# Moving four of the six modulation sums of each layer ahead of its attention heads

## The chip, the cores and the metric

One core of one Trainium2 chip. The metric is device time in microseconds (us) of one execution. Before the change: 3334.44 us, the median of 3 runs (3331.59 to 3336.16).

## The reference

Two layers, each with a token-mixing half (a stick-breaking branch and an MLA branch, 8 heads each) and a squared-ReLU MLP. S = 1024 positions, D = 1024 channels, float32. What the change touches is `mod`, six vectors of 1024 numbers per layer:

```python
for l in range(DEPTH):                                  # 2
    mod = (c_act @ w_ada[l] + b_ada[l])[:, None, :]     # (1024,) @ (1024, 6144)
    shift1, scale1, gate1, shift2, scale2, gate2 = jnp.split(mod, 6, axis=-1)
    h = _rms_norm(x, g_mix_norm[l]) * (1.0 + scale1) + shift1
    p = h @ w_in[l]                                     # q, k, v, latents, rope, gates
    ...                                                 # both attention branches
    x = x + gate1 * (merged @ w_mix_out[l])
    h = _rms_norm(x, g_mlp_norm[l]) * (1.0 + scale2) + shift2
    x = x + gate2 * (jnp.square(jax.nn.relu(h @ w_up[l])) @ w_down[l])
```

So vectors 0 and 1 are needed at the start of a layer, 2 (gate1) after its heads, 3 to 5 in its MLP. `w_ada` is 24 MB per layer, each vector 4 MB.

## The kernel before

The activations are held transposed, channels on partitions. Every product of two float32 operands is made of three passes (high x high, high x low, low x high parts), each a matmul of a 128x128 weight tile with 512 columns, into the PSUM banks `pp`. One layer runs, in program order, through these stages: the latent projections (`lraw`, `lt`); the stretch ahead of the heads, called so below (the rope key, the first q, k, v pair, gates 0 to 3, then in `for p in range(4)` the up-projections from the latents to the heads' q, k, v, and gates 4 to 7); the stick-breaking heads (scores `sc<-sq`); the MLA heads (`sc<-mq`); the output products and the mixing product (`merged`); the up-projection, a pair loop with fast products on half blocks (`pw`, results in `u`); the down-projection (`bo`, `ws`, sums in `x`).

The order on each engine isn't the program's. The code records all operations in a `Plan`; `Plan.deadlines` gives each a due time worked back from TensorE's program order, and `Plan.schedule` is a list scheduler over five engines (TensorE, ScalarE, VectorE, GpSimd, one DMA queue on SyncE) with its own durations, which writes the order out. Tiles of one class take its buffers strictly in the order in which the program makes them (`c.tiles[j] is not t` in `slots_for`). All instructions are recorded by one helper, so every row of the profile has line L213, and work is told apart by tile names.

The modulation. VectorE, not TensorE, sums `w_ada` rows weighted by the activated c: `modulation(l, parts)` is a generator that goes through the given vectors in blocks of 256 columns. A block has four loads of 256 KB into `AD` (2 buffers), two multiply-adds each into `acc` (class `A`, 3 buffers, 128 partitions x 256), eight in all, with one step of the generator per load. `finish` splits the sum into a high part (ScalarE) and a low part (GpSimd), both in class `A` too, and sums over partitions by four matmuls with two columns of ones into a bank of class `tp`, which VectorE adds to `mod`. The heads use the two `tp` banks for their transposes and outputs, and the latents' norm uses them ahead of that. The first layer's vectors 0 and 1 are made in `start` by other code (tile `ada`). Before, layer 0's vectors 2 to 5 (16 blocks, 128 multiply-adds) are stepped by `interleave`, among the heads of layer 0, and all six of layer 1 (24 blocks, 192 multiply-adds) among the pair loop and the down-projection of layer 0. Layer 1 itself carries none.

Evictions ahead of the heads: `keep_split` writes a high part (ScalarE) and a low part (VectorE) into two `lt` tiles (4 buffers, class `lt2`) and stores both; `keep` writes a `T` tile (ScalarE) and stores it; `rope` has six VectorE operations. `load_w` loads 128 columns of a weight into `raw`, ScalarE and GpSimd split it into `parts`.

Of the kernel before, what the change touches and what calls it, by code (L numbers as in the profile page):

```python
# [25 lines left out]
DEPTH = 2  # L26
# [460 lines left out]
class Trunk:  # L487
# [631 lines left out]
    def layer(self, l, xT, ssq, before):  # L1119
# [17 lines left out]
        def gate(m):  # L1137
            gd[m] = self.dt([P, S])
            return (win_w(2208 + m * P), self.keep(gd[m], AF.Sigmoid if m < 8 else AF.Copy), P)
# [23 lines left out]
        def rope(ps, sl, n, out):  # L1163

            a, b = ltmp(), ltmp()
            nc.vector.tensor_mul(a, ps, cos[:, sl])
            nc.vector.tensor_mul(b[:64], ps[64:], sin[64:, sl])
            nc.vector.tensor_mul(b[64:], ps[:64], sin[:64, sl])
            nc.vector.tensor_add(a, a, b)
            hi, lo = ltmp(F32R), ltmp(F32R)  # L1170
            nc.scalar.copy(out=hi, in_=a)
            nc.vector.tensor_sub(lo, a, bc(hi))
            for i, t in enumerate((hi, lo)):
                for r in (0, 64) if n < 64 else (0,):
                    m = n if n < 64 else P
                    o = r // 64 * n
                    nc.sync.dma_start(out=out[i, o : o + m, sl], in_=bc(t[r : r + m]))
# [56 lines left out]
        lat_norm(0, range(0, 3), QR, "g_q_lat")  # L1234
        lat_norm(1, range(3, 5), KVR, "g_kv_lat")
        kr_job = (kr_w, lambda ps, sl: rope(ps, sl, 16, kpe_d), P)
        for _ in self.linear([kr_job] + qkv(0) + [gate(m) for m in range(4)], hh, hl, KT):
            pass

        c_qp, c_lt = self.vcls("qp", 16, 17, *range(18, 24)), self.vcls("lt2", 15, 5, 6, 7)  # L1240

# [26 lines left out]
        for p in range(4):  # L1268
            mq[p], mk[p], mv[p] = self.two(), self.two(), self.dt([P, S])
            if p % 2 == 0:  # L1270
                wq = q_parts(p // 2)
            q_w = part(wq, p % 2 * P)
            for _ in self.linear([(q_w, self.keep_split(mq[p], ltmp), P)], lath, latl, 3):
                pass
            wkv = kv_parts(p)
            k_w, v_w = part(wkv, 0), part(wkv, P)
            kv_jobs = [(k_w, self.keep_split(mk[p], ltmp), P), (v_w, self.keep(mv[p]), P)]
            for _ in self.linear(kv_jobs, lath[3:], latl[3:], 2):
                pass
            if p % 2 == 0:  # L1280
                g = p // 2
                qr_d[g] = self.two()
                w = part(wq, 2 * P)()
                for sl in HALVES:
                    ps = self.bank("pp")
                    self.mm3(ps, w, lath, latl, sl, 3)
                    rope(ps, sl, 64, qr_d[g])
            for _ in self.linear([gate(4 + p)], hh, hl, KT):
                pass

        self.attention_banks()

# [67 lines left out]
        fill = [self.linear(qkv(p + 1), hh, hl, KT) for p in range(3)]  # L1360
        fill += [self.linear([gate(m) for m in range(8, 16)], hh, hl, KT)]
        fill = self.chain(fill)
        ada = self.modulation(0, [2, 3, 4, 5]) if l == 0 else iter(())
        for name, head, weights, mask, vals, steps in (
            ("sb", sb_head, self.sb_weights, self.mask_s, vd, SB_STEPS),
            ("mla", mla_head, self.mla_weights, self.mask_c, mv, MLA_STEPS),
        ):
            if name == "sb":
                self.c_q, self.c_F = self.vcls("sq", *q_slots[:6]), self.vcls("F", *q_slots[6:])
            else:  # L1370
                self.c_q = self.vcls("mq", *q_slots)
                fill = self.chain([fill, sb_out()])
            for p in range(4):
                od[name, p] = self.dt([P, S])
                a = self.attend([head(p, e) for e in range(2)], lambda: self.make_v(vals[p]), weights, mask, od[name, p])
                self.interleave(a, 19, fill, steps[p], ada)
        for _ in self.chain([fill, ada]):
            pass


# [61 lines left out]

        NP = DFF // P // 2
        hid = [self.dt([P, 8, HALF]) for m in range(NP)]
        ada = self.modulation(l + 1, range(6)) if l + 1 < DEPTH else iter(())

        def hidden(f):
            where = (0, 7) if f % 2 == 0 else (1, 2)
# [23 lines left out]
        for m in range(2, DFF // P // 2):  # L1472
            a, S3, c, d, S1, S2, S4 = self.pair_weights(I["w_up"][l, :, 2 * m * P : 2 * (m + 1) * P], c_pr, c_pw)
            u, v = self.full(c_u), self.full(c_u)
            next(ada, None)
            p1 = self.product(a, B11)
            nc.scalar.copy(out=u[:, :HALF], in_=p1)
            p6 = self.product(S2, T[2])
            nc.vector.tensor_add(u[:, HALF:], p6, u[:, :HALF])
            next(ada, None)  # L1480
            p7 = self.product(S3, T[3])
            nc.vector.tensor_add(v[:, :HALF], p7, u[:, HALF:])
            p5 = self.product(S1, T[1])
            nc.vector.tensor_add(v[:, HALF:], p5, v[:, :HALF])
            nc.vector.tensor_add(u[:, HALF:], p5, u[:, HALF:])
            next(ada, None)
            p4 = self.product(d, T[4])
            nc.vector.tensor_sub(v[:, :HALF], v[:, :HALF], p4)
            p2 = self.product(c, B21)
            nc.vector.tensor_add(u[:, :HALF], p2, u[:, :HALF])  # L1490
            next(ada, None)
            p3 = self.product(S4, B22)
            nc.vector.tensor_add(u[:, HALF:], p3, u[:, HALF:])
            for t in (v, u):
                nc.scalar.activation(out=t, in_=t, func=AF.Relu)
                nc.scalar.activation(out=t, in_=t, func=AF.Square)
            nc.sync.dma_start(out=hid[m][:, 0], in_=u[:, :HALF])
            nc.sync.dma_start(out=hid[m][:, 1:3], in_=v.rearrange("p (a b) -> p a b", a=2))
            combine(m, u, v)
            if m in (3, 5):  # L1500
                u, v = self.full(c_u), self.full(c_u)
                i = m // 2 - 1
                nc.sync.dma_start(out=u[:, :HALF], in_=hid[i][:, 0])
                nc.sync.dma_start(out=u[:, HALF:], in_=hid[i][:, 7])
                nc.sync.dma_start(out=v.rearrange("p (a b) -> p a b", a=2), in_=hid[i][:, 1:3])
                combine(i, u, v)
        ssq = [self.tmp(), self.tmp()]
        steps = self.down(l, hid, x_d, ssq)
        for _ in range(48):
            next(steps)  # L1510
            next(ada, None)
        for _ in ada:
            pass
        return self.xT, ssq, steps

    def down(self, l, hid, x_d, ssq):
# [111 lines left out]
            yield from g  # L1628

    @staticmethod  # L1630
    def interleave(a, na, b, nb, c):

        done = 0
        for i, _ in enumerate(a):
            if i % 2 == 1:
                next(c, None)
            want = (i + 1) * nb // na
            while done < want:
                next(b, None)
                done += 1  # L1640
# [69 lines left out]
```

## Time and profile before

| | |
|---|---|
| median of 3 runs | 3334.44 us |
| profiled execution | 3345.88 us |
| its span (first to last instruction) | 3344.1 us |
| TensorE busy | 3116.7 us, 93% |
| VectorE busy | 2295.3 us, 69% |
| ScalarE, GpSimd busy | 1544.1 us, 1243.2 us |
| multiply-adds of `modulation` | 320 on VectorE, from 160 loads |

The profile is of one execution; times in it are from its span's start. Busy time says how long an engine had an instruction under way; what a stage is bound by is seen from the engine that never pauses in it, and from the waits. PE is TensorE's matmuls, PEld its weight loads, DVE VectorE, ACT ScalarE, POOL GpSimd, SPq the queue of SyncE, which issues all DMAs.

### The profile page before, as it was taken

The numbers are of one execution on the slowest core, as the hardware profiler recorded it, in microseconds if no ns is written. First come the engines' busy times: TensorE is split into PE (matmuls) and PEld (weight loads), VectorE is DVE, ScalarE is ACT, GpSimd is POOL, SyncE is SP. The second block draws the span as 40 slices with busy tenths as digits, with TensorE's granted clock in tenths as the row PEclk, the third lists the DMA queues.
The fourth block names the chain that finished last, engine by engine and source line by source line (L and its number), as shares of the span: only waits on it lengthen the run. The fifth ranks groups of instructions, "written<-read, shape, count | busy, mean of one in ns | idle before, by whom it ended". The sixth has DMA issues, their size and how long they took to land.

```text
span 3344.1 us, 42801 instructions
## 1 busy us (share of the span) xinstructions
PE 3116.7 (93%) x14823; PEld 2519.9 (75%) x14823; DVE 2295.3 (69%) x3238; ACT 1544.1 (46%) x2643; POOL 1243.2 (37%) x952
## 2 busy tenths in 40 slices
PE   5999899999998989998999998999999989999998
PEld 4877677778776777776777877778887767888886
DVE  7443677768567687799986326766675777658786
ACT  4443455657344434433344335556664444444434
POOL 3222344211234654344533223442112456544542
PEclk8999999999999999999999999999999999999999
DMA  6456455545844555876333474344457436467522
GB/s 216 148 164 187 119 150 141 143 129 155 273 128 126 187 189 174 258 237 206 104 103 91 131 219 130 105 126 108 112 167 243 133 104 204 155 199 255 181 76 89
DMA packets 450268, 532.46 MB, mean 159 GB/s; under 512 B 32498, under 2 KB 320900, under 8 KB 450052
## 3 DMA queue, kind: packets, MB, share of 16 engines
q1 hardware_dynamic: 450052, 529.72, 51.8%
q8 instruction: 118, 1.93, 0.3%
q14 instruction: 98, 0.80, 0.1%
HBM read 367.60 MB, written 162.00 MB: 158 GB/s over the span
## 4 chain that ended last, share of the span: by engine, by line
PE 61%; DVE 18%; DMA 11%; issue 4%; ACT 3%; POOL 1%; SPq 1%; DVEq 0%; ACTq 0%; POOLq 0%
PE pp L213 50%; PE tp L213 7%; PE sc L213 4%; DVE A L213 4%; DVE T L213 3%; DVE F L213 3%; DMA AD<-in_w_ada 3%; DMA T<-dram 2%; DVE x L213 2%; DMA dram<-T 1%; DVE wtl L213 1%; DVE bo L213 1%; DVE u L213 1%; POOL parts L213 1%; DMA vT<-dram 1%
## 5 line engine op out<-in xcount | busy, mean ns | idle before, releaser
L213 PE MATMUL pp<-H,parts 128*128 128x512 f32 x4032 | 1060.4, 407 | 13.5 <-ACT H L213 11.4
L213 PEld LDWEIGHTS pp<-H,parts 128*128 128x128 f32 x4032 | 742.3, 191 | 165.4 <-ACT H L213 13.1
L213 PE MATMUL pp<-bo,ws 128*128 128x512 f32 x2688 | 642.4, 400 | 28.0 <-POOL ws L213 15.7
L213 POOL TENSOR_TENSOR parts<-raw,parts 128x1024 fp32r<-128x1024 f32 (+2 forms) x168 | 370.1, 2204 | 758.0 <-ACT parts L213 699.2
L213 PEld LDWEIGHTS pp<-bo,ws 128*128 128x128 f32 x2688 | 506.7, 190 | 151.0 <-POOL ws L213 18.8
L213 POOL TENSOR_TENSOR ws<-wr,ws 128x1024 fp32r<-128x1024 f32 x112 | 295.7, 2647 | 367.2 <-ACT ws L213 335.3
L213 PE MATMUL pp<-t,pw 128*128 128x512 f32 x1344 | 322.0, 397 | 9.8 <-ACT u L213 9.5
L213 PEld LDWEIGHTS pp<-t,pw 128*128 128x128 f32 x1344 | 251.0, 189 | 70.4 <-ACT u L213 10.5
L213 DVE TENSOR_TENSOR_SCAN F<-F 128x128 f32<-128x128 f32 (+7 forms) x128 | 235.4, 1848 | 90.3 <-ACT F L213 90.2
L213 ACT CAST parts<-raw 128x1024 fp32r<-128x1024 f32 (+2 forms) x168 | 151.9, 904 | 265.1 <-PE pp L213 228.0
L213 PE MATMUL pp<-b,pw 128*128 128x512 f32 x1008 | 248.6, 404 | 14.4 <-DVE u L213 14.4
L213 ACT CAST wth<-tp 128x512 fp32r<-128x512 f32 (+3 forms) x384 | 180.8, 481 | 153.1 <-PE tp L213 147.9
L213 DVE TENSOR_TENSOR wtl<-tp,wth 128x512 fp32r<-128x512 f32 (+3 forms) x384 | 205.5, 548 | 64.8 <-ACT wth L213 62.9
L213 POOL TENSOR_TENSOR W<-W,F 128x127 f32<-128x127 f32 (+7 forms) x128 | 168.6, 1321 | 210.4 <-DVE F L213 117.5
L213 DVE SCALAR_TENSOR_TENSOR x<-pp,const,x 128x512 f32<-128x512 f32 x256 | 181.7, 740 | 90.6 <-PE pp L213 90.6
L213 POOL TENSOR_TENSOR pw<-T,pw 128x512 fp32r<-128x512 f32 x112 | 165.0, 1489 | 208.5 <-ACT pw L213 208.0
L213 PEld LDWEIGHTS pp<-b,pw 128*128 128x128 f32 x1008 | 191.3, 192 | 62.0 <-DVE u L213 17.4
L213 DVE SCALAR_TENSOR_TENSOR A<-AD,const,A 128x256 f32<-128x256 f32 x280 | 211.6, 756 | 30.7 <-DMA AD<-in_w_ada 27.2
L213 PE MATMUL tp<-const,W 128*128 128x128 f32 x1152 | 187.4, 277 | 44.3 <-DVE wtl L213 34.8
L213 ACT CAST bo<-T 128x512 fp32r<-128x512 f32 x224 | 135.4, 620 | 163.6 <-DMA T<-dram 106.1
L213 PEld LDWEIGHTS tp<-const,W 128*128 128x128 f32 x1152 | 138.4, 142 | 87.3 <-DVE wtl L213 26.0
L213 DVE TENSOR_TENSOR bo<-T,bo 128x512 fp32r<-128x512 f32 x224 | 192.1, 904 | 15.6 <-ACT bo L213 15.2
(151 smaller groups left out, 4614.5 us busy)
## 6 DMA issues: line engine op xcount, KB each, us to landing
T<-dram SPq DMA_DIRECT2D x352, 256.0 KB
dram<-T SPq DMA_DIRECT2D x208, 256.0 KB
dram<-u SPq DMA_DIRECT2D x92, 512.0 KB
AD<-in_w_ada SPq DMA_DIRECT2D x160, 256.0 KB
raw<-in_w_in SPq DMA_DIRECT2D x70, 512.0 KB
wr<-in_w_down SPq DMA_DIRECT2D x64, 512.0 KB
pr<-in_w_up SPq DMA_DIRECT2D x56, 512.0 KB
sq<-dram SPq DMA_DIRECT2D x96, 256.0 KB
```

Source lines behind the costliest of these rows:

```text
L213: getattr(getattr(nc, engine), method)(*[r(x) for x in a], **{n: r(x) for n, x in k.items()})
```

## The change

`modulation(l, [2, 3, 4, 5])` is made for both layers just ahead of the first linear job after the latents' norm, and stepped by the loops of the stretch ahead of the heads: two steps for each half job of the first block of linears and of each gate, one for the others, and what is left at the end (76 steps are offered for 64). `interleave` loses its third generator. The MLP of layer 0 steps only `modulation(1, range(2))`, three times per pair instead of four, and finishes it ahead of the down-projection's steps.

```diff
+        ada = self.modulation(l, [2, 3, 4, 5])
         for _ in self.linear([kr_job] + qkv(0) + [gate(m) for m in range(4)], hh, hl, KT):
-            pass
+            next(ada, None)
+            next(ada, None)
...
             for _ in self.linear([(q_w, self.keep_split(mq[p], ltmp), P)], lath, latl, 3):
-                pass
+                next(ada, None)
...
             for _ in self.linear(kv_jobs, lath[3:], latl[3:], 2):
-                pass
+                next(ada, None)
...
                     rope(ps, sl, 64, qr_d[g])
+                    next(ada, None)
             for _ in self.linear([gate(4 + p)], hh, hl, KT):
-                pass
+                next(ada, None)
+                next(ada, None)
+        for _ in ada:
+            pass
...
-        ada = self.modulation(0, [2, 3, 4, 5]) if l == 0 else iter(())
...
-                self.interleave(a, 19, fill, steps[p], ada)
-        for _ in self.chain([fill, ada]):
+                self.interleave(a, 19, fill, steps[p])
+        for _ in fill:
             pass
...
-        ada = self.modulation(l + 1, range(6)) if l + 1 < DEPTH else iter(())
+        ada = self.modulation(l + 1, range(2)) if l + 1 < DEPTH else iter(())
...
             nc.vector.tensor_add(u[:, HALF:], p5, u[:, HALF:])
-            next(ada, None)
             p4 = self.product(d, T[4])
...
         steps = self.down(l, hid, x_d, ssq)
+        for _ in ada:
+            pass
         for _ in range(48):
             next(steps)
-            next(ada, None)
-        for _ in ada:
-            pass
```

What it does to the order is seen on two engines, both in layer 0's stretch ahead of the heads. First VectorE, where the stretch's first up-projections are evicted (`lt<-pp,lt` is the low part of an eviction, `lt<-pp,cs` the first operation of a rope). Before:

```order
L213 TENSOR_TENSOR lt_1546<-lt_1510,lt_1541 128x512
L213 TENSOR_TENSOR lt_319_1690<-pp_1668,lt_318_1685 128x512
L213 TENSOR_TENSOR lt_322_1708<-pp_1683,lt_321_1703 128x512
L213 TENSOR_TENSOR lt_328_1735<-pp_1701,lt_327_1717 128x512
L213 TENSOR_TENSOR lt_331_1751<-pp_1713,lt_330_1742 128x512
L213 TENSOR_TENSOR lt_338_1773<-pp_1749,cs_1184 128x512
```

And with the change, the same five evictions:

```order
L213 SCALAR_TENSOR_TENSOR A_1748<-AD_1770,const_98,A_1748 128x256
L213 TENSOR_TENSOR lt_380_1805<-pp_1774,lt_379_1793 128x512
L213 SCALAR_TENSOR_TENSOR A_1748<-AD_1770,const_98,A_1748 128x256
L213 TENSOR_TENSOR lt_387_1822<-pp_1791,lt_386_1815 128x512
L213 TENSOR_SCALAR A_1836<-AD_1796,const_98 128x256
L213 SCALAR_TENSOR_TENSOR A_1836<-AD_1796,const_98,A_1836 128x256
L213 TENSOR_TENSOR const_277<-tp_1828,const_252 128x2
L213 SCALAR_TENSOR_TENSOR A_1836<-AD_1830,const_98,A_1836 128x256 x2
L213 TENSOR_TENSOR lt_395_1871<-pp_1813,lt_394_1838 128x512
L213 SCALAR_TENSOR_TENSOR A_1836<-AD_1854,const_98,A_1836 128x256 x2
L213 TENSOR_TENSOR lt_399_1899<-pp_1832,lt_398_1882 128x512
L213 TENSOR_TENSOR lt_413_1908<-pp_1877,cs_1184 128x512
```

Between evictions now stand one to five operations of the sums, each pair of which needs a load. The second place is SyncE's queue at the same evictions. Before, it holds their stores (`dram<-lt`) and the next weights:

```order
L213 DMA dram_1729<-lt_327_1717 128x512
L213 DMA dram_1729<-lt_328_1735 128x512
L213 DMA dram_1729<-lt_330_1742 128x512
L213 DMA dram_1729<-lt_331_1751 128x512
L213 DMA dram_1768<-T_1737 128x512
L213 DMA raw_1777<-in_w_q_up 128x2x384
```

With the change:

```order
L213 DMA AD_1830<-in_w_ada 128x2x256
L213 DMA dram_1802<-lt_380_1805 128x512
L213 DMA dram_1802<-lt_386_1815 128x512
L213 DMA AD_1854<-in_w_ada 128x2x256
L213 DMA dram_1802<-lt_387_1822 128x512
L213 DMA dram_1868<-lt_394_1838 128x512
L213 DMA AD_1879<-in_w_ada 128x2x256
L213 DMA dram_1868<-lt_395_1871 128x512
L213 DMA dram_1868<-lt_398_1882 128x512
L213 DMA AD_1906<-in_w_ada 128x2x256
L213 DMA dram_1868<-lt_399_1899 128x512
L213 DMA raw_1920<-in_w_q_up 128x2x384
```

A load of the sums now stands behind every second store, and each store behind a load that needs a free `AD` buffer.

On TensorE, the 64 small matmuls of a layer's 16 blocks stand, counted in the new order, behind the 608th to the 1234th other matmul in layer 0 and the 7694th to the 8332nd in layer 1; before, those of layer 0 stood behind the 1384th to the 3683rd. On VectorE, 48 multiply-adds stay in the pair loop and 16 stand in the down-projection of layer 0. The 16 of layer 0's first two blocks stand in its start in both orders, and 16 stand around the mixing product in both.

## Rows read from the trace of the kernel before

**Rows 1.** The page: busy time by engine, and the last chain by line.

```profile
PE 3116.7 (93%) x14823; PEld 2519.9 (75%) x14823; DVE 2295.3 (69%) x3238; ACT 1544.1 (46%) x2643; POOL 1243.2 (37%) x952
...
PE pp L213 50%; PE tp L213 7%; PE sc L213 4%; DVE A L213 4%; DVE T L213 3%; DVE F L213 3%; DMA AD<-in_w_ada 3%; DMA T<-dram 2%; DVE x L213 2%; DMA dram<-T 1%; DVE wtl L213 1%; DVE bo L213 1%; DVE u L213 1%; POOL parts L213 1%; DMA vT<-dram 1%
```

**Rows 2.** Busy time by stage, layer 0 then layer 1; columns in the first line.

```profile
core 0: us, PE busy (x) PEld busy (x) DVE busy (x) ACT busy (x) POOL busy (x), PEclk, DMA share, GB/s
173.00:303.00 130.00, 130.00 (x562) 105.11 (x561) 45.72 (x66) 44.25 (x80) 32.68 (x33) 1.00 0.59 180
303.30:610.30 307.00, 267.51 (x1469) 213.68 (x1468) 218.26 (x270) 158.00 (x304) 131.31 (x141) 0.97 0.51 140
610.30:831.50 221.20, 209.95 (x1302) 178.86 (x1301) 168.04 (x429) 145.28 (x324) 33.42 (x80) 0.98 0.53 144
1084.10:1395.40 311.30, 288.69 (x1229) 231.78 (x1228) 230.36 (x321) 126.08 (x187) 154.28 (x112) 0.97 0.58 190
1395.40:1700.10 304.70, 281.76 (x1198) 224.81 (x1197) 282.80 (x340) 116.03 (x166) 140.98 (x59) 0.98 0.57 183
1838.00:2001.00 163.00, 162.51 (x700) 130.94 (x700) 47.14 (x70) 48.69 (x86) 38.49 (x36) 1.00 0.55 168
2001.10:2291.80 290.70, 262.41 (x1474) 212.17 (x1473) 192.22 (x212) 156.28 (x301) 123.52 (x140) 0.98 0.45 123
2291.80:2489.00 197.20, 196.30 (x1229) 167.17 (x1227) 142.47 (x357) 140.70 (x311) 27.57 (x66) 1.00 0.48 126
2735.10:3010.60 275.50, 273.90 (x1177) 220.21 (x1176) 170.10 (x220) 126.38 (x179) 148.74 (x100) 1.00 0.54 179
3010.60:3278.20 267.60, 267.60 (x1158) 216.70 (x1157) 219.88 (x241) 111.69 (x151) 124.04 (x47) 1.00 0.53 167
```

**Rows 3.** VectorE's longest waits, 1838 to 2001 us: total, times, longest.

```profile
DVE lt L213 <- ACT lt L213: 89.0, 16, 50.1
```

**Rows 4.** The same columns for the sums alone (tile A), layer 0.

```profile
173.00:303.00 130.00, 0.00 (x0) 0.00 (x0) 0.00 (x0) 0.00 (x0) 0.00 (x0) 1.00 0.59 180
303.30:610.30 307.00, 6.46 (x31) 6.12 (x31) 36.60 (x56) 3.29 (x8) 7.85 (x7) 0.97 0.51 140
610.30:831.50 221.20, 5.47 (x33) 5.32 (x33) 26.43 (x56) 2.88 (x7) 6.15 (x8) 0.98 0.53 144
1084.10:1395.40 311.30, 8.37 (x51) 9.81 (x51) 78.79 (x92) 4.68 (x12) 8.94 (x12) 0.97 0.58 190
1395.40:1700.10 304.70, 7.48 (x45) 8.36 (x45) 83.54 (x84) 4.46 (x11) 13.98 (x11) 0.98 0.57 183
```

**Rows 5.** Timeline of TensorE's weight loads, 1400 to 1413 us.

```profile
1400.74 0.19 PEld L213 LDWEIGHTS tp<-const,A 128*128 128x128 f32 x1
...
1406.43 0.19 PEld L213 LDWEIGHTS tp<-const,A 128*128 128x128 f32 x1
...
1412.12 0.19 PEld L213 LDWEIGHTS tp<-const,A 128*128 128x128 f32 x1
```

**Rows 6.** Busy time of the down-projection's products (tile bo), layer 1.

```profile
3010.60:3278.20 267.60, 267.19 (x1152) 216.04 (x1151) 88.56 (x96) 57.39 (x94) 1.00 0.53 167
```

**Rows 7.** Tile A: its multiply-adds, durations in ns (min/median/max).

```profile
L213 DVE SCALAR_TENSOR_TENSOR A<-AD,const,A x280: 453/484/2683, 34.3 to 1658.8; 128x256 f32<-128x256 f32 x140
```

**Rows 8.** Timeline of SyncE's queue, 618 to 637 us: start, length, what.

```profile
618.82 0.38 SPq L213 DMA_DIRECT2D AD<-in_w_ada  x1
...
624.10 1.61 SPq L213 DMA_DIRECT2D AD<-in_w_ada  x2
```

**Rows 9.** The same view, 1181 to 1234 us.

```profile
1222.76 0.37 SPq L213 DMA_DIRECT2D AD<-in_w_ada  x1
...
1230.37 0.45 SPq L213 DMA_DIRECT2D AD<-in_w_ada  x1
```

**Rows 10.** The last chain in order of time: start, us, what.

```profile
549.31 2.71 DMA AD<-in_w_ada
...
634.60 5.95 DMA AD<-in_w_ada
663.79 7.10 DMA AD<-in_w_ada
```

More of the change, by code (lines that the diff above doesn't have):

```diff
@@ L1630, in interleave @@
     @staticmethod
-    def interleave(a, na, b, nb, c):
+    def interleave(a, na, b, nb):
         done = 0
         for i, _ in enumerate(a):
-            if i % 2 == 1:
-                next(c, None)
             want = (i + 1) * nb // na
```

## The prediction

> **What bounds the kernel now.** I began with the busy shares and the chain of work that ended last. TensorE is busy 93% of the span, but half of the chain only is the plain products (`PE pp`); the sums of the modulation (`DVE A`, the multiply-adds) and their loads (`DMA AD<-in_w_ada`) hold 4% and 3% of it [rows 1]. So they end waits somewhere, though they are 128x256 operations of half a microsecond. To see where, I used that the two layers do the same work in the same order, and that only layer 0's attention, up- and down-projection carry these sums: the second layer is the first without them. The busy times by stage [rows 2] are cut at the first product that reads each stage's own operands (the heads' q and k tiles, then `pw`, then `bo`). In the heads TensorE has the same number of matmuls in both layers (1469 + 1302, of which 64 are those of the sums, against 1474 + 1229), yet layer 0 needs 307.0 and 221.2 us where layer 1 needs 290.7 and 197.2. The up-projection's pair loop takes 311.3 against 275.5, the first 1152 products of the down-projection 304.7 against 267.6. In layer 1 these last two have TensorE at 99 to 100%. The reader is to see that in layer 0 the stall is VectorE's: it is busy 71, 76, 74 and 93% there. Ahead of the heads, by contrast, TensorE does not pause at all (130.0 of 130.0 us, 162.5 of 163.0), and VectorE works 35% and 29% of the time. One of its waits there lasts 50.1 us in layer 1 [rows 3].
>
> **What is removed.** In the heads of layer 0, 112 multiply-adds (56 + 56) [rows 4]. Difference of the layers: 307.0 + 221.2 - 290.7 - 197.2 = 40.3 us, 0.36 us each. In the pair loop 92 cost 311.3 - 275.5 = 35.8 us, 0.39 each; in the down-projection 84 cost 37.1 us, 0.44 each. The new order still has 48 in the pair loop (six of the eight blocks of the two vectors) and 16 in the down-projection (the first two blocks of layer 1's own four are pulled ahead that far, since only a third needs a free buffer). So 44 x 0.39 = 17.1 and 68 x 0.44 = 30.0 are saved. **Saved: 40.3 + 17.1 + 30.0 = 87.4 us.** If what is left costs nothing, 40.3 + 35.8 + 37.1 = 113; if the two loops lose as much to half as many, 40.3 + 30.0 = 70. The 16 multiply-adds in the start and the 16 around the mixing product stay where they are.
>
> **What is added.** Each layer's stretch ahead of the heads gets 112 multiply-adds, 56 loads of 256 KB, 14 casts and 14 subtractions, and 64 matmuls of two columns.
>
> *TensorE.* The stretch is TensorE's, so its part is paid in full. In the down-projection of layer 0 one weight load of such a matmul comes every 5.69 us (1400.74, 1406.43, 1412.12), with 24 wide matmuls between [rows 5]. Without them 24 wide ones take 24 x 267.60 / 1152 = 5.575 us [rows 6]. That is 0.115 us each; at least nothing, at most the 0.19 of the weight load. 128 x 0.115 = **14.7 us**, bounds 0 and 24.
>
> *VectorE.* 112 multiply-adds a layer. Their means differ by stage: 36.60/56 = 0.65 us, 0.47, 0.86, 0.99 [rows 4], and follow how busy GpSimd is (43, 15, 50, 46%) [rows 2]; the shortest is 0.453, the longest 2.683 us [rows 7]. Ahead of the heads GpSimd is busy 25 and 24%, so I take 0.55: 62 us a layer, on top of 46 and 47. VectorE is then busy about 108 of some 150 us, no more than in layer 1's heads (142 of 197), where TensorE runs at 99.5%. So its busy time alone hides. The Trainium skill ("SBUF — State Buffer", section on who interferes with whom) says that a VectorE operation with two SBUF inputs and a GpSimd operation that reads SBUF take a shared port in turn, each for its whole length. The long rows agree; by that rule the sums become cheaper by moving to where GpSimd is quiet, and at the 0.99 of the down-projection they would come to 111 us a layer instead.
>
> *The chain of loads.* This is the doubtful term. `AD` has two buffers, so a buffer is loaded, read by two multiply-adds, and loaded again; a block of 256 columns needs four loads, two rounds. What had 520 us in the heads and 600 in the MLP must now finish in about 150 a layer, because the result goes through the `tp` banks in program order, and the heads' first transposes stand behind it. In the new order the blocks are 626/15 = 41.7 wide matmuls apart in layer 0 and 638/15 = 42.5 in layer 1, at 0.2323 us [rows 6] and with four small matmuls 10.1 and 10.3 us. So the round may take 5.1 us; whatever is above it stops TensorE at the block's small matmuls, twice per block, for 14 blocks (the first two are summed in the start, or in the down-projection). Measured rounds: 618.82 to 624.10, 5.3 us, in the MLA heads with GpSimd at 15% [rows 8]; 1222.76 to 1230.37, 7.6 us, in the pair loop with GpSimd at 50% [rows 9]. At 25% and with free VectorE time behind each landing I take 5.5, nearer the first: blocks of 11.0, 14 x 0.9 + 14 x 0.7 = 22 us. Lower end 0 (rounds of 5.1), upper end 14 x (15.2 - 10.1 + 15.2 - 10.3) = 140 us at 7.6.
>
> The loads stand in SyncE's one queue among the stores of the stretch and the next weights, so when a load waits for its buffer, the stores behind it wait, and the `lt` tiles that these free come late for the next eviction. Four `pp` banks and a second pair of weight buffers are the cover; I charge nothing beyond the rounds. The bytes fit: 180 GB/s x 130 us = 23.4 MB, with 14.7 MB more 38 MB in 150 us, 254 GB/s; the DMA share rises from 0.59 to about 0.84 (180 GB/s / 0.59 = 305 at full share).
>
> **Sum.** -87.4 + 14.7 + 22 = -51 us. The profiled execution took 3345.88 us (span 3344.10), 11 above the median; the change is the same on both. **Forecast: 3334.44 - 51 = 3283 us.** About 0.2%, 6.7 us, is what a measurement of this kernel tells from no change.
>
> **Rivals.**
> *The loads land late* (the other side). Where the chain shows them, a load takes 2.71 us from issue to use when quiet, 5.95 and 7.10 us in the MLA heads at a DMA share of 0.53 [rows 2, 10]. Ahead of the heads the share would be 0.84. If the mean landing moves from some 3.2 to 4.7, rounds are 7.0, blocks 14.0: 14 x (3.9 + 3.7) = 106 us lost, and -87 + 15 + 106 = +34: 3368 us. It decides from rounds of 6.3 us on, where 14 x (2.5 + 2.3) = 67 and the small matmuls eat the gain. Against it: two loads are in flight, and longer stretches lower the share again. The Trainium skill ("DMA: Bandwidth & Descriptors", section on latency and other measured facts) gives HBM access as 0.2 us on average and 2 us at high load, which speaks for this rival. Chance 0.14.
>
> *The sums cost the same everywhere.* If each moved multiply-add costs TensorE its 0.36 to 0.44 us ahead of the heads too, because evictions queue behind it on VectorE, 224 x 0.39 = 87 us come back: 3334, no change. Against it: VectorE has 65 to 71% idle time there, and the evictions have four banks. Chance 0.06.
>
> *The loops lose all of their stall.* If six blocks in the pair loop and two in the down-projection hide in VectorE's gaps, 113 are saved, and with rounds of 5.2 us (14 x 0.3 + 14 x 0.1 = 6) and the small matmuls 113 - 15 - 6 = 92: 3242 us. For it: layer 1's loop leaves VectorE 38% idle. Against it: the loss per multiply-add is the same at 0.36 to 0.44 in stages of unlike load. Chance 0.12.
>
> **How the numbers follow.** The forecast has 0.68. Its own range: rounds of 5.1 give -73 (3262), rounds of 6.2 give -87 + 15 + 61 = -11 (3323). The range reaches half way into the larger gain (3250) and just to the edge of the late loads (3330): 3250 to 3330. Faster 0.68 + 0.12 = 0.80, the same 0.06, slower 0.14.
>
> **What would show it.** Right: layer 0's heads take 291 + 197 us within 5, no `A` operation among them beyond the first 15 us; the down-projection's first 1152 products take about 275; ahead of the heads TensorE falls from 100% to some 90% and waits at `tp<-const,A`. Wrong in the main: TensorE waits there for `pp` products whose weights or banks are late, or the stretch grows by over 45 us in a layer, or the heads start with a stall because the `tp` banks still belong to the sums.

## The result, and the profile after

With the change the kernel takes 3291.73 us, the median of 4 runs (3288.95 to 3306.77), beside 3333.02 (3324.14 to 3336.16, 4 runs) before, on the same chip: ratio 0.989, 95% interval 0.9854 to 0.9925, or 25 to 49 us less. The forecast was 3283, its range 3250 to 3330. By the medians the kernel gained 41 us. The profiled execution took 3292.37 us, span 3290.6, which is 53.5 us less than the profiled one of before; but that one was 11 us above its median, so the stages below, read from these two executions, show more gain than the medians do.

The page's busy times, that answer to the first of [rows 1]:

```profile
PE 3096.3 (94%) x14823; PEld 2505.4 (76%) x14823; DVE 2312.3 (70%) x3238; ACT 1547.5 (47%) x2643; POOL 1237.9 (38%) x952
```

The work is the same and its busy time hardly differs; what moved is where engines wait. Before, the two stretches ahead of the heads, from the first transpose of the latents to the heads' first product, read

```profile
153.00:303.30 150.30, 149.82 (x645) 120.67 (x644) 62.99 (x90) 57.37 (x98) 37.49 (x35) 1.00 0.58 178
1819.20:2001.10 181.90, 180.67 (x776) 144.83 (x774) 64.42 (x95) 57.10 (x100) 42.87 (x38) 1.00 0.52 158
```

With the change, the table of stages is this. The first two lines are the stretches ahead of the heads of layer 0 and 1, then layer 0's heads in two parts, its pair loop and the first 1152 products of its down-projection, and last the first part of layer 1's heads; but for the stretches they are cut as in [rows 2]:

```profile
153.40:334.80 181.40, 165.44 (x701) 130.08 (x700) 122.43 (x207) 62.87 (x111) 47.88 (x48) 0.96 0.71 219
1754.80:1959.30 204.50, 194.25 (x840) 155.12 (x839) 127.72 (x224) 62.60 (x116) 55.37 (x53) 0.97 0.70 215
334.80:622.50 287.70, 259.76 (x1481) 209.74 (x1481) 197.00 (x224) 157.53 (x303) 124.58 (x142) 0.99 0.46 129
622.50:818.60 196.10, 196.10 (x1231) 167.49 (x1230) 142.70 (x358) 141.10 (x312) 27.52 (x66) 1.00 0.48 127
1063.90:1358.20 294.30, 282.13 (x1209) 227.86 (x1208) 196.89 (x277) 127.49 (x186) 151.18 (x107) 0.98 0.56 186
1358.20:1636.00 277.80, 270.08 (x1152) 216.67 (x1151) 248.79 (x256) 109.79 (x152) 129.25 (x48) 0.99 0.52 166
1959.30:2242.60 283.30, 259.00 (x1474) 210.54 (x1473) 192.93 (x212) 156.56 (x301) 123.35 (x140) 0.99 0.44 123
```

The heads of layer 0 went from 307.0 + 221.2 us to 287.7 + 196.1 (44.4 saved), the pair loop from 311.3 to 294.3 (17.0), the first 1152 products from 304.5 (304.7 in [rows 2]) to 277.8 (26.7). The two stretches ahead of the heads, in which TensorE was idle for 0.5 and 1.2 us before, are 31.1 and 22.6 us longer; TensorE is idle for 16.0 and 10.3 us in them, at a granted clock of 0.96 and 0.97. Not forecast were 4.2 us less in layer 0's mixing product and 11.7 less in layer 1's heads, where the change moves nothing (290.7 + 288.5 to the mixing product before, 283.3 + 284.2 now). All of it: 31.1 + 22.6 - 44.4 - 17.0 - 26.7 - 4.2 - 11.7 = -50; the other 3 are in stages that I don't follow.

What the longer stretches wait for stands among their waits (us in total, times, longest), first in layer 0's, then in layer 1's:

```profile
DVE A L213 <- DMA AD<-in_w_ada: 40.0, 28, 4.2
...
PEld tp L213 <- ACT A L213: 17.6, 10, 3.7
...
PE tp L213 <- ACT A L213: 13.2, 9, 3.2
...
DVE A L213 <- DMA AD<-in_w_ada: 42.4, 29, 5.0
...
PEld tp L213 <- ACT A L213: 12.9, 9, 3.1
...
PE tp L213 <- ACT A L213: 9.5, 8, 2.7
```

Most of TensorE's idle time there (13.2 of 16.0 us and 9.5 of 10.3, by the rows of the matmuls, PE; the weight loads', PEld, are longer) is one wait: its small matmuls `tp<-const,A` stand behind ScalarE's cast of a finished sum, and that behind VectorE, and VectorE behind loads. Products waited for a late eviction only once, 1.9 us in layer 0. How the main wait looks once, in the timeline of layer 0's stretch:

```profile
239.50 1.00 DVE L213 SCALAR_TENSOR_TENSOR A<-AD,const,A 128x256 f32<-128x256 f32 x2
...
240.59 0.41 ACT L213 CAST A<-A 128x256 fp32r<-128x256 f32 x1 [2.48 <-DVE A L213]
...
241.05 0.19 PEld L213 LDWEIGHTS tp<-const,A 128*128 128x128 f32 x1 [1.61 <-ACT A L213]
```

The last two multiply-adds of a block end at 240.50, the cast at 241.00, and TensorE, idle for over a microsecond, goes on at 241.05.

### The profile page after: what moved, and what is told of

Read it like the earlier page. It is cut to its first block, busy times and chain, and to the rows that moved or that the text cites. A ratio compares the mean times of both kernels' runs of the same rounds, so it can differ in the third digit from the quotient of the medians.

```text
span 3290.6 us, 42871 instructions
## 1 busy us (share of the span) xinstructions
PE 3096.3 (94%) x14823; PEld 2505.4 (76%) x14823; DVE 2312.3 (70%) x3238; ACT 1547.5 (47%) x2643; POOL 1237.9 (38%) x952
## 5 line engine op out<-in xcount | busy, mean ns | idle before, releaser
L213 PE MATMUL pp<-bo,ws 128*128 128x512 f32 x2688 | 631.1, 396 | 13.7 <-DVE bo L213 5.0
L213 PEld LDWEIGHTS pp<-t,pw 128*128 128x128 f32 x1344 | 252.5, 189 | 71.4 <-ACT u L213 11.2
L213 DVE SCALAR_TENSOR_TENSOR A<-AD,const,A 128x256 f32<-128x256 f32 x280 | 184.2, 658 | 79.8 <-DMA AD<-in_w_ada 74.7
L213 DVE TENSOR_TENSOR bo<-T,bo 128x512 fp32r<-128x512 f32 x224 | 215.1, 1008 | 17.0 <-ACT bo L213 16.7
L213 ACT CAST ws<-wr 128x1024 fp32r<-128x1024 f32 x112 | 117.0, 1049 | 190.3 <-PE pp L213 168.8
```

What stands on the lines that cost most here:

```text
L213: getattr(getattr(nc, engine), method)(*[r(x) for x in a], **{n: r(x) for n, x in k.items()})
```

## The experiments

All times are medians; ratios are to the kernel before, run on the same chip. The kernels ran on several chips, where the one before took 3333.02 to 3339.59 us, so a difference of medians between chips can be off by 7 us; where it matters, the difference by ratios stands beside it. I read each by its stretches ahead of the heads, beside the whole time. The stretches are of one execution and one order each. The control below has the same sums and loads as the changed kernel, and its stretches still differ by 3.6 and 2.5 us, so prices read from one stretch are good to some 4 us. One table for all:

| kernel | us | ratio, 95% interval | stretch, layer 0 | layer 1 |
|---|---|---|---|---|
| before | 3333.02 | 1 | 150.3 | 181.9 |
| after | 3291.73 | 0.989 (0.9854 to 0.9925) | 181.4 | 204.5 |
| four buffers | 3279.34 | 0.9826 (0.9807 to 0.9845) | 171.0 | 196.3 |
| its control | 3291.76 | 0.9862 (0.9842 to 0.9881) | 185.0 | 202.0 |
| one load only | 3275.18 | 0.9807 (0.9782 to 0.9831) | 169.5 | 192.9 |
| no sums | 3241.87 | 0.971 (0.9688 to 0.9731) | 150.7 | 181.1 |
| small matmuls alone | 3256.68 | 0.9746 (0.973 to 0.9763) | 158.1 | 188.1 |
| layer 0 alone | 3327.44 | 0.9964 (0.9952 to 0.9977) | 178.0 | 181.9 |
| layer 1 alone | 3312.09 | 0.9919 (0.9906 to 0.9932) | 150.4 | 206.7 |
| one buffer | 3330.91 | 0.9982 (0.9965 to 0.9998) | 171.8 | 200.2 |
| float32 columns | 3296.4 | 0.9879 (0.986 to 0.9899) | 182.6 | 198.0 |
| the same, four buffers | 3283.93 | 0.9834 (0.9818 to 0.9851) | 172.5 | 192.3 |
| planner's numbers | 3271.2 | 0.9808 (0.9791 to 0.9825) | 163.4 | 195.0 |
| the same, four buffers | 3258.05 | 0.9776 (0.9757 to 0.9794) | 167.0 | 193.0 |

### What the sums cost ahead of the heads, taken apart

Three kernels each leave out more of the moved sums. In the first, all sums of a stretch read one load, so every block sums the same rows. In the second the four vectors are the bias alone: no sums ahead of the heads, and none of their first blocks in the start and the down-projection. The third has the small matmuls back, on constant tiles, with no load and no multiply-add.

```diff
# one load only
+                    if not once or (k0 == 0 and c0 == 0 and m == parts[0]):
-                    w = self.tile(self.AD, [P, 2, 256])
+                        w = self.tile(self.AD, [P, 2, 256])
...
-                    nc.sync.dma_start(out=w, in_=cols(v))
+                        nc.sync.dma_start(out=w, in_=cols(v))
# no sums
+        if len(parts) == 4:
+            nc.vector.tensor_copy(out=self.mod[l][:, 16:48], in_=self.v(l, "b_ada", 32, 16))
+            self.mod_finish(l, 4)
+            return
# small matmuls alone: as above, but for each block of 256 columns
+                    for j in range(2):
+                        for i, t in enumerate((hi, lo)):
+                            nc.tensor.matmul(
+                                ps[:, 2 * j : 2 * j + 2], t[:, j * P : (j + 1) * P], self.ones[:, :2], start=i == 0, stop=i == 1
+                            )
```

> The changed kernel, where the sums ahead of the heads read one resident tile, loaded once per layer, instead of 64 loads; all multiply-adds, casts and small matmuls stay (the values of vectors 2 to 5 are therefore those of repeated rows). Theory, rounds of loads: of the growth of 31.5 and 22.4 us only the small matmuls (7.4 each) and a few us stay: 3291.7 - 34 = about 3258 us (3250 to 3268). Rival, VectorE's time and queue: 3284 to 3294.

> The changed kernel without the sums of vectors 2 to 5 (they are the bias alone): no loads, multiply-adds or small matmuls ahead of the heads, and none of the 16 in the start, nor the 16 in the down-projection. It gives the whole price of the sums where the change puts them. Both theories: the stretches shrink back by 31.5 and 22.4 us, the down-projection by up to 10: 3291.7 - 60 = about 3232 us (3222 to 3245). The difference to the run with a resident tile is what VectorE's work and the small matmuls cost: by the theory of rounds about 20 to 25 us, by the rival 45 or more.

> The kernel without the loads and multiply-adds of vectors 2 to 5 (their values are not the reference's), but with their 64 small matmuls per layer ahead of the heads, on two tiles that are made once. It separates the small matmuls themselves from waiting for the sums that they read. Against the run without any of it (3242): by the prediction's price of 0.115 us, 128 x 0.115 = +15, 3257 us (3252 to 3262). If the 33 us between that run and the one with a resident tile are all small matmuls: 3272 or more. If they are VectorE's queue and the waits at the small matmuls: 3242 to 3249.

The stretches in the table of stages, layer 0 ahead of layer 1; no sums, then small matmuls alone, then one load only:

```profile
149.60:300.30 150.70, 150.19 (x646) 120.52 (x645) 62.89 (x90) 57.40 (x99) 37.42 (x35) 1.00 0.58 178
1711.00:1892.10 181.10, 180.37 (x775) 144.86 (x774) 64.58 (x95) 57.10 (x100) 43.27 (x38) 1.00 0.51 160
```

```profile
151.10:309.20 158.10, 157.09 (x710) 127.82 (x708) 66.22 (x107) 57.54 (x98) 36.86 (x35) 1.00 0.55 170
1732.60:1920.70 188.10, 187.38 (x840) 152.25 (x839) 67.24 (x112) 57.23 (x101) 42.77 (x38) 1.00 0.51 154
```

```profile
154.00:323.50 169.50, 161.58 (x710) 127.93 (x710) 125.37 (x220) 63.43 (x114) 50.50 (x50) 0.99 0.51 159
1735.60:1928.50 192.90, 188.83 (x840) 151.70 (x839) 126.67 (x224) 62.10 (x115) 55.81 (x53) 1.00 0.49 148
```

The kernel without sums falls in its range, 50 us below the changed one (60 by the ratios). The price of the new place is 30.7 + 23.4 = 54.1 us in the stretches. The small matmuls hold 7.4 + 7.0 = 14.4 of it (158.1 - 150.7, 188.1 - 181.1), with TensorE idle for 1.0 and 0.7 us only, which is close to the forecast's 0.115 us each. The kernel with one load came to 3275, between the two theories by the medians (by the ratios it is 28 us under the changed kernel, inside the first one's range), so I go by the stretches: the multiply-adds, with their casts and subtractions, cost 11.4 + 4.8 = 16.2 us with every operand resident (169.5 - 158.1, 192.9 - 188.1), and the loads 11.9 + 11.6 = 23.5 on top (181.4 - 169.5, 204.5 - 192.9).

### Where the multiply-adds cost TensorE time without any load

They are charged nothing in the prediction, since VectorE is busy for some third of the stretch before. That share is a mean. Cut into 6 us, VectorE in layer 0's stretch of before is full at first and then empty; the four lines are 166 to 172, 178 to 184, 190 to 196 and 196 to 202 us:

```profile
166.00:172.00 6.00, 5.52 (x24) 4.19 (x23) 6.00 (x8) 3.98 (x8) 2.41 (x1) 1.00 0.46 128
...
178.00:184.00 6.00, 6.00 (x27) 4.88 (x26) 5.94 (x8) 3.16 (x4) 2.40 (x1) 1.00 0.32 94
...
190.00:196.00 6.00, 6.00 (x28) 4.82 (x27) 4.60 (x6) 2.43 (x7) 4.41 (x5) 1.00 0.38 110
196.00:202.00 6.00, 6.00 (x28) 4.85 (x27) 0.00 (x0) 1.20 (x3) 1.59 (x4) 1.00 0.72 189
```

The latents' norm and low parts (`lraw<-lraw,const,lt`, `ll<-lraw,lh`) and the first evictions are made there. With the change, the four slices from 178 to 202 us read

```profile
178.00:184.00 6.00, 6.00 (x28) 4.88 (x27) 5.94 (x8) 3.36 (x4) 2.86 (x1) 1.00 0.00 0
184.00:190.00 6.00, 6.00 (x27) 4.84 (x26) 5.82 (x12) 2.37 (x5) 0.00 (x0) 1.00 0.79 242
190.00:196.00 6.00, 2.54 (x10) 1.65 (x9) 6.00 (x8) 2.76 (x6) 5.07 (x5) 0.89 0.39 124
196.00:202.00 6.00, 6.00 (x16) 4.66 (x16) 5.90 (x9) 0.80 (x4) 3.39 (x4) 0.54 0.34 108
```

VectorE is full until 202, and the first block that is summed in the stretch stands in that queue; TensorE, whose program order has the block's small matmuls there, is busy for 2.54 of 6 us. SyncE's queue stands behind VectorE as well, for 8.8 us up to a load of the sums at 183.67 (DMA share 0.00 from 178 to 184 us). The timeline of the changed kernel shows the end of that wait, and one of the sums beside a long GpSimd operation:

```profile
193.18 0.41 ACT L213 CAST A<-A 128x256 fp32r<-128x256 f32 x1 [2.79 <-DVE A L213]
...
193.64 0.19 PEld L213 LDWEIGHTS tp<-const,A 128*128 128x128 f32 x1 [3.66 <-ACT A L213]
...
194.86 2.82 POOL L213 TENSOR_TENSOR parts<-raw,parts 128x1024 fp32r<-128x1024 f32 x1
...
195.37 2.46 DVE L213 TENSOR_SCALAR A<-AD,const 128x256 f32<-128x256 f32 x1
```

Part of what fills VectorE there is the length of the sums themselves. From 166 to 202 us they are

```profile
L213 DVE SCALAR_TENSOR_TENSOR A<-AD,const,A 128x256 f32<-128x256 f32 x10 | 8.5, 850 | 0.2 <-DMA AD<-in_w_ada 0.2
```

850 ns in the mean beside a median of 485. How much of the pause that makes, no run tells.

After that pause the granted clock is 0.54 for 6 us: the lower level, 1.2 GHz, and 16 matmuls take the time of 28. The kernel with one load has a pause at the same place, so it doesn't need the loads. From 190 to 202 us it runs 37 matmuls, at a granted clock of 0.86, where the small matmuls alone let 55 through; the 18 that are missing, at the 0.218 us that one takes there (12.00/55), are 3.9 of its 11.4 us:

```profile
190.00:202.00 12.00, 9.62 (x37) 7.80 (x38) 11.94 (x16) 3.51 (x8) 8.08 (x8) 0.86 0.18 53
```

```profile
190.00:202.00 12.00, 12.00 (x55) 9.79 (x55) 4.72 (x6) 3.72 (x9) 3.84 (x6) 1.00 0.51 137
```

I put the remainder down to shorter waits of the same kind later on: with this pause there are 11.2 us in 10 waits of `PEld tp` for `ACT A` in layer 0, 4.1 in layer 1. Another wait lies in the same chain. With the loads gone, VectorE waits in layer 0 for 10.0 us, in 9 waits, behind GpSimd's subtractions, whose tiles share the three buffers of class `A` with the sums. No run gives that class more buffers; the one with four load buffers and float32 matmuls (below) makes no cast and no subtraction, has no such wait, and its stretches are 172.5 and 192.3 us beside 171.0 and 196.3, so without this wait nothing is won in layer 0, and 4.0 us in layer 1.

### More and fewer buffers for the loads

With four buffers for `AD` two rounds of a block needn't wait for each other. The two more come from the class of the weights' high and low parts, so the control takes these away alone. One buffer is the other direction.

```diff
# four buffers (ahead of the heads alone)
+        c_ad = self.cls("AD", ["ad0", "ad1", *(self.V[i] for i in more)])   # more = (22, 23)
-        c_qp, c_lt = self.vcls("qp", 16, 17, *range(18, 24)), self.vcls("lt2", 15, 5, 6, 7)
+        c_qp, c_lt = self.vcls("qp", 16, 17, *range(18, 22)), self.vcls("lt2", 15, 5, 6, 7)
# control: the qp line alone
# one buffer (ahead of the heads alone)
+        c_ad = self.cls("AD", ["ad0", "ad1"][:n])                           # n = 1
```

> The changed kernel with four load buffers for the sums ahead of the heads (two more taken from the q weights' class, which keeps six of eight). Theory, rounds of loads: the stretch ahead of the heads grew by 31.5 us in layer 0 and 22.4 in layer 1 because a buffer comes round only every 6.0 and 5.5 us; with four, VectorE's waits for these loads (43 us per layer) fall below 20 and TensorE's waits at the small matmuls (about 22 and 13 us) mostly go: 3291.7 - 25 = about 3267 us (3257 to 3278). Rival, VectorE's queue: the evictions stand behind the sums however early the loads land: 3285 to 3298. A third case: the scheduler uses the buffers to pack the sums closer, and the stretch stays as long.

> The changed kernel with the q weights' class at six buffers, nothing else: the control for the run with four load buffers. Both theories: 3291.7 within 7 us. If it is slower, the price belongs to those buffers and is to be taken off that run.

> The changed kernel with one load buffer instead of two ahead of the heads: the suspected cost made larger. Theory, rounds of loads: a load and its two multiply-adds then take turns, some 2.7 + 1.1 + 0.4 = 4.2 us per load, 17 us per block against 12.0 and 11.0 now: 14 x 5 + 14 x 6 = +154 us, about 3446 us (3400 to 3480). Rival, VectorE's queue or the small matmuls: the work on VectorE and TensorE is the same, so under +30 us.

The control shows no loss: 3291.76 us, with a ratio whose interval overlaps that of the changed kernel. Four buffers, run on the control's chip, take 12 us off it, half of what I expected. Beside the changed kernel 10.4 and 8.2 us come back in the stretches (14.0 and 5.7 beside the control). VectorE no longer waits for loads (3.2 us in place of 40.0), but TensorE still waits, as long as with one load only:

```profile
PEld tp L213 <- ACT A L213: 11.7, 10, 3.9
...
DVE A L213 <- DMA AD<-in_w_ada: 3.2, 4, 1.4
```

So the loads' part of the price is real and about as large as in the subtraction (18.6 of 23.5), and the remaining wait is for VectorE's sums.

One buffer missed its number by far: 39 us more (31 by the ratios), not 154. I had doubled each round at a fixed place of the small matmuls. But the scheduler knows of the one buffer and lets other work go ahead. 55 multiply-adds now stand behind the heads' first product (10 in the changed kernel); the `A` operations from there to the MLA heads' first product:

```profile
331.10:665.80 334.70, 4.42 (x28) 4.50 (x28) 35.68 (x55) 2.83 (x7) 5.14 (x7) 0.98 0.46 130
```

The first part of the heads is 334.7 us long for it, and the rest to the mixing product 255.3 in place of 283.8, since products have come forward from it (1626 and 1492 matmuls, 1481 and 1617 in the changed kernel). Layer 1's heads are longer too, 319.3 + 278.3 us in place of 283.3 + 284.2. The direction holds, the pricing doesn't: a late sum moves work about before it stops TensorE.

### The two layers apart

```diff
# layer 0 alone; layer 1's sums stay in layer 0's MLP, six vectors as before
+        ada = self.modulation(l, [2, 3, 4, 5]) if l == 0 else iter(())
# layer 1 alone; layer 0's stay in its heads, interleaved as before
+        ada = self.modulation(l, [2, 3, 4, 5]) if l == 1 else iter(())
```

> Layer 0's part of the change alone: its four vectors ahead of its heads, layer 1's six in layer 0's MLP as before. By the stages of the two traces: heads -19.3 and -25.1, stretch ahead of them +31.5, a few us back in the output products: before - 16 us, about 3317 (3309 to 3326). By the prediction's sum (-40.3 + 7.4 + 13): before - 20. If the two halves are independent, this and the other half add up to -41.

> Layer 1's part of the change alone: layer 0's four vectors among its heads as before, layer 1's last four ahead of its own heads. By the stages of the two traces: pair loop -17.2, down-projection -26.6, layer 1's stretch +22.4, its heads -7: before - 27 us, about 3306 (3297 to 3315). By the prediction's sum (-17.1 - 30.0 + 7.4 + 9): before - 31.

Layer 0 alone gives 11 us by the medians, layer 1 alone 26, together 37, beside 41 for both: no part of the gain needs the other. The first is 5 us short of its forecast (-16), the second met it (-27). Layer 0's move pays little because the stretch gives 27.7 of the 42.3 us back that heads and what follows to the mixing product win (307.0 + 312.0 to 292.1 + 284.6).

### Fewer small matmuls

One float32 matmul of one column per half block, on the sum itself, in place of two of two columns on its high and low parts; no cast, no subtraction.

```diff
-            hi, lo = (self.tile(self.A, [P, 256], F32R) for _ in range(2))
-            nc.scalar.copy(out=hi, in_=acc)
-            nc.gpsimd.tensor_sub(lo, acc, bc(hi))
...
+                nc.tensor.matmul(
+                    ps[:, 2 * j : 2 * j + 1], acc[:, j * P : (j + 1) * P], bc(self.ones[:, :1]), start=True, stop=True
+                )
```

> The changed kernel, where a block's sum over partitions is two float32 matmuls with one column, as the start does it, instead of a cast, a subtraction and four matmuls on split parts. Theory: 160 - 80 fewer small matmuls, 64 of them ahead of the heads at 0.12 to 0.15 us (8 to 10 us), and the wait of TensorE for cast and subtraction behind the last multiply-add (about 1.2 us of each block) goes in part: 3291.7 - 15 = about 3277 us (3268 to 3284). Rival: a float32 weight load of this shape costs as much as the two it replaces, and the waits are for the last multiply-add, not for the cast: 3287 to 3297.

> Four load buffers and the two float32 matmuls together. If the two causes, rounds of loads and the block's end, are independent, their gains add: -12 and -15, about 3265 us (3256 to 3274). If both only shorten the same wait at the small matmuls, it is no better than the better of the two, about 3277.

Neither gains, as the rivals had it: 3296 beside 3292, and with four buffers 3284 beside 3279. The trace says why the small matmuls got no cheaper. The program has 80 such matmuls, the trace twice as many weight loads of 128x128 and as many matmuls:

```profile
L213 PEld LDWEIGHTS tp<-const,A x160: 186/188/338, 172.2 to 1935.1; 128*128 128x128 f32 x160
L213 PE MATMUL tp<-const,A x160: 164/250/353, 172.5 to 1935.1; 128*128 128x1 f32 x160
```

So a float32 matmul of this form shows as two weight loads and two matmuls, and nothing was left out there. That the cast and the subtraction are gone from the chain isn't seen in the time either: layer 1's stretch is 6.5 and 4.0 us shorter, but layer 0's is not, and the down-projection of the first is 7.4 us longer (285.2 for 277.8, with 24 multiply-adds there for 16).

### The planner's numbers

The list scheduler plans a multiply-add at 0.40 us, where the trace has 0.56 to 0.61. This gives it 0.56, and 1.2 us more to the landing of a load of `w_ada`, with two buffers and with four.

```diff
+        op.late = 1.2 if op.eng == "DMA" and "AD" in names else 0.0
+        if op.eng == "DVE" and "AD" in names:
+            op.dur = 0.56
...
-        return LAT[p.eng] + (TO_PE if o.eng == "PE" else 0.0)
+        return LAT[p.eng] + p.late + (TO_PE if o.eng == "PE" else 0.0)
```

> The changed kernel with another two numbers in the scheduler: 0.56 us for a multiply-add of the sums (the traces' mean ahead of the heads; its own cost function gives 0.40) and 1.2 us more until a load of the sums has landed. Nothing else changes; the small matmuls then stand about 55 wide matmuls apart instead of 41, and the last blocks fall among the heads. Theory, planned too early: TensorE waits at the small matmuls because they are placed for sums that VectorE cannot have ready: those waits (some 21 and 13 us) fall below 10 in all, the stretches shrink by 12 and 8 us, and the heads lose up to 10 by the later end: 3291.7 - 12 = about 3280 us (3270 to 3290). Rival, the sums' own pace: TensorE then waits with its transposes in the heads for the same time: 3288 to 3300.

> The same two numbers in the scheduler with four load buffers. The blocks stand some 34 wide matmuls apart (7.9 us of TensorE) and end ahead of the heads. Theory, planned too early: against four buffers alone (3279) the waits at the small matmuls, still 12 us in layer 0, mostly go: 3279 - 10 = about 3269 us (3262 to 3275). Rival: those waits are VectorE's own pace, 8 multiply-adds of 0.56 and the evictions between them, which no order changes: 3276 to 3284.

By the medians the first is in its range, though beyond the 12 us of its theory, and the second is below its range: 21 us under the changed kernel (27 by the ratios, (0.989 - 0.9808) x 3333) and 21 under four buffers (17 by the ratios). With four buffers it is the fastest version that makes all sums, 3258 us, 0.9776 of before. The pause at 190 to 202 us is all but gone (49 matmuls, clock 1.00):

```profile
190.00:202.00 12.00, 11.09 (x49) 8.76 (x50) 10.05 (x16) 3.87 (x10) 7.50 (x8) 1.00 0.51 158
```

and TensorE's waits for a cast sum in that stretch fell from 11.7 to 6.9 us:

```profile
PEld tp L217 <- ACT A L217: 6.9, 9, 2.2
```

But this confirms the theory in part alone: beside four buffers the stretches are only 4.0 and 3.3 us shorter. 9.9 of the gain are in the pair loop (295.1 to 285.2) and 2.2 in the down-projection, where 48 and 16 multiply-adds got the new numbers as well. With two buffers the stretch of layer 0 is 163.4, but 7.7 of its 18.0 us come back in the first part of the heads (295.4).

## Why the prediction was right, step by step

**What is removed** held in its sum. Layer 0's heads saved 44.4 us against 40.3, the pair loop 17.0 against 17.1, the down-projection 26.7 against 30.0: 88.1 for 87.4. The difference of the layers is a good price for what all sums of a stage cost, and the pair loop, which keeps half of its sums, kept half of its stall, so the rival *the loops lose all of their stall* (pair loop 275.5) fell there: it stayed 18 us above layer 1's loop.

A price for each multiply-add that is left does not come out of the runs. With the same 48, the pair loop takes 285.2 (planner's numbers) to 295.4 us (layer 1 alone). The first 1152 products of the down-projection take 266.8 (one load) to 277.8 us with 16 multiply-adds, and about as long in the two kernels that have none there, 271.4 (no sums) and 274.0 (small matmuls alone); the first line is no sums, the second planner's numbers with four buffers:

```profile
1321.00:1592.40 271.40, 268.92 (x1153) 217.16 (x1152) 227.90 (x242) 111.11 (x153) 126.22 (x47) 0.99 0.50 161
...
1333.70:1600.80 267.10, 267.10 (x1153) 216.11 (x1151) 229.34 (x256) 111.57 (x151) 127.08 (x48) 1.00 0.54 172
```

So that 68 of 84 gone gave 26.7 us there, near 68 x 0.44, is in part luck: in the order of the planner's numbers, with the same 16 left, 37.6 are gone, all of the stall. Nor is the stall in that stage VectorE's by the waits, as the prediction has it: there TensorE waited before mostly for GpSimd's parts of the weights,

```profile
PE pp L213 <- POOL ws L213: 15.7, 7, 5.1
```

of 22.9 us idle, and 0.2 us for VectorE itself. Why the sums lengthen that wait stays open.

**TensorE's small matmuls** held: 14.4 us for 14.7, measured with none of the loads and multiply-adds in the stretch.

**The chain of loads** held in its sum, 23.5 us against 22. The rounds answer to the forecast of 5.5 (the row gives first and last of a stretch's load issues, layer 0 ahead of layer 1):

```profile
L213 SPq DMA_DIRECT2D AD<-in_w_ada x54: 367/383/1045, 183.7 to 345.1; - x54
...
L213 SPq DMA_DIRECT2D AD<-in_w_ada x54: 367/383/646, 1785.8 to 1937.3; - x54
```

Two loads are a round, and 54 issues span 26.5 rounds: (345.1 - 183.7)/26.5 = 6.1 us in layer 0, which includes the first pause, and (1937.3 - 1785.8)/26.5 = 5.7 in layer 1. The rival *the loads land late* needed 6.3 and more, and a DMA share of 0.84; it was 0.71 and 0.70 in stretches longer than the 150 us that it was worked out for. The composition was not foreseen. Beside the kernel where one load serves all, TensorE is idle 8.0 and 6.2 us longer, and busy 3.9 and 5.4 us longer for the same wide matmuls, at a granted clock of 0.96 and 0.97 in place of 0.99 and 1.00. So some two fifths of the loads' price, 9.3 of 23.5 us, is TensorE running slower, not TensorE waiting.

**VectorE** is the step that failed: "So its busy time alone hides", charged 0, measured 16.2 us. The size of one multiply-add was right. With the change they take this long in the rest of each stretch (busy times of the `A` operations alone, layer 0 from 167 us, layer 1 from 1793):

```profile
167.00:334.80 167.80, 9.24 (x56) 9.23 (x56) 62.72 (x102) 5.28 (x13) 10.49 (x13) 0.96 0.73 222
...
1793.00:1959.30 166.30, 9.89 (x57) 11.40 (x57) 59.13 (x106) 5.69 (x14) 10.79 (x14) 0.97 0.78 240
```

62.72/102 = 0.61 and 59.13/106 = 0.56 us, against 0.55. What was wrong, as the slices show, was to set 108 us of work against a mean of 150: the idle time isn't spread over the stretch, and a small matmul waits for its own block. That the scheduler's 0.40 puts the blocks too early is borne out by the shorter waits of the last experiments, not proven, since these changed other orders as well.

The rival *the sums cost the same everywhere* is out: 224 of them cost 39.7 us ahead of the heads without their small matmuls (54.1 - 14.4), 0.18 each, not 0.39.

The unforeseen price of 16 us was nearly met by an unforeseen gain of 15.9 in layer 0's mixing product and layer 1's heads (4.2 + 11.7). That is why the sum of -51 stands beside a span of -53.5; it is partly luck. By the medians the kernel gained 41 us, 10 less than the sum, and the -51 lies just outside the measured interval of 25 to 49. The heads of layer 1 are shorter in the kernels whose stretch ahead of them is longer (290.5 us for 181.1, 287.1 for 196.3, 283.3 for 204.5), as if the scheduler filled waits there with products that the heads would else carry. No run tests that, and not every kernel follows it (286.4 for 206.7 with layer 1 alone, 291.0 for 195.0 with the planner's numbers), so the cause stays open.

## What to carry to other kernels

Where a stage runs once with some side work and once without, the difference prices the stall of all of that work, and each of three stages here came within 5 us of the forecast made from it; it doesn't price a part of the work, since the order alone moved a loop by 10 us. The new place needs its own price, made of the work that the bounding engine gets (14 us), the rounds of few buffers (24 us) and the queue of the engine that does the work (16 us). Look at an engine's idle time in slices of a few microseconds, not as a share of the stage: VectorE's 35% was 6.00 and 5.94 of 6 us in slices just where the first sums went. A list scheduler wants measured durations of what it places: two numbers in its costs and two free tiles as buffers were worth 34 us more than the change alone (3258 beside 3292).

## What the runs showed of the hardware

A pause of TensorE of some 3.5 us was followed by 6 us at a granted clock of 0.54, 16 matmuls instead of 28: 12 missing ones at 0.218 us are 2.6 us more, so this pause was paid nearly twice. Not every wait did that: behind one of 1.9 us, in 232 to 238 us, the clock stayed at 1.00. A stretch with ten waits, of 1.8 us in the mean, ran at 0.96. A float32 matmul with one column shows as two weight loads and two matmuls (160 rows for 80). A VectorE operation with one SBUF input that takes 0.35 us in the median (`TENSOR_SCALAR A<-AD,const`) took 2.46 beside a GpSimd operation of 2.82 us.
